# Weighted sums of attention heads made two pairs at a time in a hybrid decoder layer

## Chip, cores and metric

The kernel runs on one core of a Trainium2 chip. The metric is the device time of one execution in microseconds (us); before the change it is 390.96 us, the median of three runs (390.86 to 391.17).

## What is computed

One decoder layer over 512 positions of width 1024 in fp32. The input is normalized and projected to the queries, keys, values and gate paths of two attention branches, and to two merge gates. Branch A (8 heads of 64) is a block-sparse softmax attention with a relative bias; branch B (8 heads of 64) is stick-breaking attention. Each branch's output is multiplied by SiLU of its gate path, projected up to 1024, weighted with a sigmoid merge gate, and the sum goes through an output projection to which the input is added. Cut to what matters here:

```
oa = moba_attention(qa, ka, va, rel_bias)      # softmax weights x va, per head
ob = stick_breaking_attention(qb, kb, vb)      # stick-breaking weights x vb, per head
ya = (merge_heads(oa) * silu(za)) @ w_up_moba
yb = (merge_heads(ob) * silu(zb)) @ w_up_sb
y = sigmoid(gl_a) * ya + sigmoid(gl_b) * yb
x = x + y @ w_out
```

The change concerns the products "weights x values" of the heads, their place in the order of the work, and nothing of what they compute.

## The kernel before

The dense projections are products of fp32 split into a high and a low part, three matmuls for each piece (`mm3`, lines 177 to 181). The start of the kernel projects qa, ka, va and vb, row by row. From there on the main loop (lines 601 to 622) goes over eight pairs of heads, `PAIRS`: m = 0 to 3 are branch A, m = 4 to 7 branch B.

For a pair m the loop issues, in this order:

- `scores` (lines 407 to 421): 24 matmuls per pair for the two heads, 64 rows of the array each, so that the two heads stand side by side in the array (tile shape 64*128 in the profile). They go to six banks of PSUM of the kind "s".
- from m = 2 on, `finish(m - 1, "pj")`: the weighted sum of the pair before, in a bank of the kind "pj".
- for each of the two heads: `softmax` or `stick` on ScalarE (ACT) and VectorE (DVE), then `turn` (32x32 transposes on VectorE), `put` (four DMAs to DRAM), a `fill`, and `get` (a DMA back to SBUF, issued by ScalarE, into one of four buffers `pt`).
- two more `fill`s, with `finish(0)` between them at m = 1.

A `fill` takes the next entry of a list written out by hand (`FILLS`, lines 46 to 54): chunks of the dense projections, 24 matmuls over the whole array each (`chunk_ct`, lines 398 to 404), or a piece of branch A's up projection. They keep TensorE at work while a head's weights are made and turned. A fill's bank is of the kind "pj" where its tag says so; the first two fills of each m always are. Behind the last pair come two fills, `finish(7)`, one more fill, and branch B's up projection `up("b", c)`, which needs all of branch B's sums.

`finish(m, tag)` (lines 595 to 599) is `weighted` and `split_o`. `weighted` (lines 480 to 492) takes one bank `po`, issues eight matmuls, which the profile shows as 16, with 128 rows and 64 columns of the array each (tile shape 128*64), again the two heads side by side, and then one VectorE multiplication (line 491) that reads the bank and multiplies by SiLU of the gate path. `split_o` (lines 518 to 523) makes the high part on ScalarE (line 522) and the low part on VectorE (line 523). A finish issues no DMA.

There are two banks of the kind "pj" and six of the kind "s":

```python
BANKS = {"pj": 2, "s": 6}
...
def bank(tag, name):
    return pp.tile([P, S], F32, tag=tag, bufs=BANKS[tag], name=name)
```

A bank is used again only when whatever reads its last content is done. The framework puts each engine's instructions in a fixed order when the kernel is built: of those that are ready by its own reckoning of the times, the one that comes first in the source. On the chip each engine goes through its list in that order. So an instruction can stand behind others that come after it in the source.

Of the kernel before, what the change touches and what calls it, by code (L numbers as in the profile page):

```python
# [57 lines left out]
def hybrid_layer(ctx: ExitStack, tc: tile.TileContext, x, xT, w, rel, out):  # L58
# [40 lines left out]
    def sum_w(names, done):  # L99

        with tc.issue_after(G.tensor_copy(turn_of, done[:1, :1].bitcast(F32)).ins):  # L101
            for n in range(2):
                for name in names:
                    if n == 0:
                        sums[name] = vp.tile([P, H // 2, 2, P], F32, tag="v", name=name).rearrange("p a b d -> p (a b d)")
                    blk = TERMS[name[:2]][n]
                    src = sums[blk + name[2]] if blk[0] == "T" else w[WO + BLOCKS.index(blk + name[2])]
                    nc.gpsimd.dma_start(sums[name], src, **({"accum_op": ALU.add} if n else {}))
# [165 lines left out]
    def load_bias(h):  # L274
        bt = oms[2 + h % 2][:, :S]
        nc.sync.dma_start(bt, bass.AP(tensor=e_dr.tensor, offset=e_dr.offset + h * TW, ap=[[1, P], [1, S]]))
        return bt
# [129 lines left out]
    def scores(br, p, q, k, res):  # L407

        (qh, ql), (kh, kl) = q[p], k[p]
        for grp in ((3,), (2,), (1, 0)):  # L410
            ps = [bank("s", f"s{br}{2 * p + b}{grp[0]}") for b in range(2)]
            c = 0
            for i in grp:
                n = (i + 1) * P
                for m, (x, y) in enumerate(((qh, kl), (ql, kh), (qh, kh))):
                    for b in range(2):
                        o = slice(b * HD, (b + 1) * HD)
                        T.matmul(ps[b][:, c:c + n], x[o, i * P:(i + 1) * P], y[o, :n], start=m == 0, stop=m == 2)  # L418
                for b in range(2):
                    res[2 * p + b][i] = ps[b][:, c:c + n]  # L420
                c += n
# [32 lines left out]
    def turn(br, h, rows):  # L454
        turned = tp.tile([P, 4, BLK[-1], 32], F32, tag="turned", bufs=2, name=f"turned{br}{h}")
        for i in (3, 2, 1, 0):
            for j in range(0, i + 1, 2):
                n = min(2, i + 1 - j)
                step = (BLK[j + 1] - 1 - BLK[j]) if n == 2 else 1
                at = BLK[j] + i - j  # L460
                V.transpose(turned[:, :, at:at + (n - 1) * step + 1:step, :].rearrange("p q j r -> p j q r"),  # L461
                            rows[i][:, j * P:(j + n) * P].rearrange("p (j q c) -> p j q c", j=n, q=4))
        return turned

    def put(br, h, turned):
        dr = dp.tile([P, 4 * PQ], F32, tag="pd", bufs=4, name=f"pd{br}{h}")
        for a in range(4):
            nc.sync.dma_start(bass.AP(tensor=dr.tensor, offset=dr.offset + a * PQ,
                                      ap=[[4 * PQ, 32], [32 * 4 * PQ, 4], [1, PQ]]),
                              turned[a * 32:(a + 1) * 32].rearrange("c q k r -> c q (k r)"))  # L470
        return dr

    def get(br, h, dr):
        pt = tp.tile([P, 4 * PQ], F32, tag="pt", bufs=4, name=f"pt{br}{h}")
        nc.scalar.dma_start(pt, dr)
        return pt
# [3 lines left out]
    def weighted(tag, br, p, vv, pts):  # L480

        po = bank(tag, f"po{br}{p}")
        for j in range(NT):
            for b in range(2):
                o, c = slice(b * HD, (b + 1) * HD), (2 * p + b) * HD
                src = pts[b].rearrange("p (a n) -> p a n", a=4)[:, :, BLK[j] * 32:BLK[j + 1] * 32]
                T.matmul(po[o, :].rearrange("p (a n) -> p a n", a=4)[:, :, j * 32:], vv[j][:, c:c + HD], src,  # L487
                         start=j == 0, stop=j == NT - 1, skip_group_check=True)
        ocol[br, p] = u = slot(f"o{br}{p}")
        dst, z = (by_block((mirror if br == "a" else blocks)(x)) for x in (u, zr[br, p]))  # L490
        V.tensor_tensor(dst, po.rearrange("p (a i r) -> p a i r", a=4, i=4).rearrange("p a i r -> p i a r"), z,
                        op=ALU.mult)
# [25 lines left out]
    def split_o(br, p):  # L518
        u = ocol[br, p]
        oH[br, p] = slot(f"oh{br}{p}", F32R)  # L520
        oL[br, p] = slot(f"ol{br}{p}", F32R)
        A.activation(oH[br, p], u, AF.Copy)
        V.tensor_tensor(oL[br, p], u, oH[br, p].bitcast(F32), op=ALU.subtract)
# [59 lines left out]
    def fill(tag="pj"):  # L583

        home[0] = tag
        for kind, i in fills.pop(0):
            make[kind](i)

    PAIRS = [("a", p) for p in range(H // 2)] + [("b", p) for p in range(H // 2)]
    done = {}  # L590

    def head(m, b):
        return PAIRS[m][0], 2 * PAIRS[m][1] + b

    def finish(m, tag="s"):

        br, p = PAIRS[m]
        weighted(tag, br, p, v_of[br], [done.pop((m, b)) for b in range(2)])
        split_o(br, p)

    for m, (br, p) in enumerate(PAIRS):
        q, k = (qa, ka) if br == "a" else (qb, kb)
        sc, rw = {h: [None] * NT for h in (2 * p, 2 * p + 1)}, {h: [None] * NT for h in (2 * p, 2 * p + 1)}
        scores(br, p, q, k, sc)
        if m > 1:
            finish(m - 1, "pj")
        for b in range(2):
            h = 2 * p + b
            bias = load_bias(h) if br == "a" else None
            (softmax if br == "a" else stick)(h, sc[h], rw[h], bias, (3, 2, 1, 0))  # L610
            done[m, b] = put(br, h, turn(br, h, rw[h]))
            fill()
            if not b:
                done[m, 0] = get(*head(m, 0), done[m, 0])
        for b in range(2):
            if m == 1 and not b:
                finish(0)
            if not b:
                done[m, 1] = get(*head(m, 1), done[m, 1])
            if (m, b) in SUMS:  # L620
                sum_w(SUMS[m, b], done[m, b])
            fill("pj" if b or not fills[1] and m < len(PAIRS) - 1 else "s")
    fill()
    fill("s")
    finish(len(PAIRS) - 1)
    fill()
    assert not fills
# [163 lines left out]
```

## Time and profile before

| | |
|---|---|
| median of three runs | 390.96 us (390.86 to 391.17) |
| the profiled execution | 391.4 us, its span 389.6 us |
| TensorE matmul busy | 385.0 us, 99% of the span |
| VectorE busy | 266.8 us, 68% |
| ScalarE busy | 194.6 us, 50% |
| granted TensorE clock, mean | 0.999 |
| DMA, mean over the span | 203 GB/s |

Times in rows are microseconds from the span's start. PE is TensorE's matmuls, PEld its weight loads, DVE VectorE, ACT ScalarE. The ends of matmuls are modelled, so the time that a matmul costs is read from the start of one to the start of the next. In a timeline, a row is start, duration, engine, line, operation, result and operands, array tile, shape and count of merged instructions; in brackets the engine's idle time before it and what ended that.

### The profile page before, as it was taken

To read this page: it belongs to the slowest core of one execution; us is meant where nothing else is said; L and a number is where in the kernel's file an instruction comes from. 1 tells how busy PE (TensorE), PEld (TensorE's weight loads), DVE (VectorE), ACT (ScalarE), POOL (GpSimd) and SP (SyncE) were. 2 spreads that over 40 slices of the span, in tenths; PEclk is the share of its full clock that TensorE was granted. 3 is DMA by queue.
4 is the path that set the end of the run, shared out by engine and by line. 5 is a ranking of instruction groups with operands and counts; after the bars stand their busy time and mean duration, and the time that the engine had idled before them with its cause. 6 is when DMAs were issued, how large, how long until landed. Compare 5 with 4: busy or idle time off the path is not lost.

```text
span 389.6 us, 5321 instructions
## 1 busy us (share of the span) xinstructions
PE 385.0 (99%) x1853; PEld 308.8 (79%) x1853; DVE 266.8 (68%) x535; ACT 194.6 (50%) x341; POOL 51.9 (13%) x100
## 2 busy tenths in 40 slices
PE   8999999999999999999999999999999999999996
PEld 5888888888887878878788878878878878888885
DVE  4824995854879477295596398489459534999962
ACT  5684522945778466264552472363254232359540
POOL 1018966000000000000000100100000000232110
PEclk9999999999999999999999999999999999999999
DMA  7977259982496946827526776776772842798935
GB/s 266 330 269 241 112 157 290 307 273 73 133 259 226 295 178 151 306 74 240 175 68 192 257 202 182 246 205 170 263 215 67 271 148 89 217 245 301 196 76 175
DMA packets 36091, 79.29 MB, mean 203 GB/s; under 512 B 3929, under 2 KB 16729, under 8 KB 36065
## 3 DMA queue, kind: packets, MB, share of 16 engines
q1 hardware_dynamic: 29584, 56.68, 45.0%
q0 software_dynamic: 2880, 9.44, 10.6%
q10 hardware_dynamic: 3600, 12.85, 9.9%
q8 instruction: 14, 0.23, 0.2%
q14 instruction: 13, 0.10, 0.1%
HBM read 62.15 MB, written 14.70 MB: 197 GB/s over the span
## 4 chain that ended last, share of the span: by engine, by line
PE 99%; DVE 0%; issue 0%
PE gl L179 8%; PE gl L181 7%; PE gl L180 7%; PE poa L487 2%; PE pob L487 2%; PE sb L418 2%; PE sa L418 2%; PE za L179 2%; PE kb L179 2%; PE zb L179 2%; PE za L180 2%; PE kb L181 2%; PE zb L181 2%; PE zb L180 2%; PE yb L181 2%; PE yb L180 2%
## 5 line engine op out<-in xcount | busy, mean ns | idle before, releaser
L140 DVE TENSOR_TENSOR wl<-wr,wh 128x1024 fp32r<-128x1024 f32 (+1 forms) x64 | 75.8, 1185 | 62.1 <-ACT wh L138 57.0
L138 ACT ACTIVATE wh<-wr 128x1024 fp32r<-128x1024 f32 (+1 forms) x64 | 65.8, 1028 | 41.4 <-DMA wr<-in_w 15.8
L179 PE MATMUL gl<-xl,wh 128*128 128x512 f32 x128 | 50.5, 395 | 0.0
L181 PE MATMUL gl<-xh,wh 128*128 128x512 f32 x128 | 49.9, 390 | 0.0
L180 PE MATMUL gl<-xh,wl 128*128 128x512 f32 x128 | 49.8, 389 | 0.0
L513 ACT ACTIVATE gl<-gl,x 128x512 f32<-128x512 f32 x16 | 11.0, 690 | 41.7 <-PE gl L181 41.6
L179 PEld LDWEIGHTS gl<-xl,wh 128*128 128x128 f32 x128 | 24.0, 188 | 5.8 <-issue 1.0
L101 POOL COPY turn_of<-ptb 1x1 f32<-1x1 f32 x3 | 1.3, 433 | 202.0 <-DMA ptb<-pdb 202.0
L181 PEld LDWEIGHTS gl<-xh,wh 128*128 128x128 f32 x128 | 24.0, 188 | 5.1
L180 PEld LDWEIGHTS gl<-xh,wl 128*128 128x128 f32 x128 | 24.0, 188 | 4.8
L446 DVE TENSOR_TENSOR_SCAN sx<-om,begin 128x512 f32<-128x512 f32 (+3 forms) x32 | 24.9, 805 | 0.2 <-ACT om L442 0.2
L430 ACT ACTIVATE pa<-pa,m 128x512 f32<-128x512 f32 (+3 forms) x32 | 17.8, 557 | 10.9 <-DVE m L428 9.0
L428 DVE CUSTOM_DVE_ANT_0 pa<-sa,om 128x512 f32<-128x512 f32 (+3 forms) x32 | 14.8, 477 | 10.9 <-PE sa L418 10.9
L461 DVE STREAM_TRANSPOSE turneda<-pa 128x256 f32<-128x256 f32 (+1 forms) x48 | 16.4, 376 | 0.1
L442 ACT ACTIVATE om<-sb 128x512 f32<-128x512 f32 (+3 forms) x32 | 14.6, 462 | 3.2 <-DVE sx L446 2.9
L461 DVE STREAM_TRANSPOSE turnedb<-pb 128x256 f32<-128x256 f32 (+1 forms) x48 | 15.9, 370 | 0.0
L444 ACT ACTIVATE pb<-sb 128x512 f32<-128x512 f32 (+3 forms) x32 | 14.7, 465 | 0.0
L448 DVE TENSOR_TENSOR pb<-pb,sx 128x512 f32<-128x512 f32 (+3 forms) x32 | 14.2, 471 | 0.0
L179 PE MATMUL za<-xl,wh 128*128 128x512 f32 x32 | 12.7, 396 | 0.0
L179 PE MATMUL kb<-xl,wh 128*128 128x512 f32 x32 | 12.6, 393 | 0.0
L179 PE MATMUL zb<-xl,wh 128*128 128x512 f32 x32 | 12.6, 393 | 0.0
L181 PE MATMUL zb<-xh,wh 128*128 128x512 f32 x32 | 12.5, 390 | 0.0
(305 smaller groups left out, 957.9 us busy)
## 6 DMA issues: line engine op xcount, KB each, us to landing
wr<-in_w SPq DMA_DIRECT2D x60, 512.0 KB, 5.4
pda<-turneda SPq DMA_DIRECT2D x32, 160.0 KB, 2.6
pta<-pda ACTq DMA_DIRECT2D x8, 640.0 KB, 6.0
pdb<-turnedb SPq DMA_DIRECT2D x32, 160.0 KB, 2.7
ptb<-pdb ACTq DMA_DIRECT2D x8, 640.0 KB, 4.5
xn<-in_x SPq DMA_DIRECT2D x8, 256.0 KB, 6.6
xs<-in_xT SPq DMA_DIRECT2D x8, 256.0 KB, 6.2
om<-e_dr SPq DMA_DIRECT2D x8, 256.0 KB, 6.5
```

Source lines behind the costliest of these rows:

```text
L138: A.activation(hi[:, a:b], raw[:, a:b], AF.Copy)
L140: low[c] = V.tensor_tensor(lo[:, a:b], raw[:, a:b], hi[:, a:b].bitcast(F32), op=ALU.subtract).ins
L179: T.matmul(ps, aH, bL, start=start, stop=False, skip_group_check=on)
L180: T.matmul(ps, aL, bH, start=False, stop=False, skip_group_check=on)
L181: T.matmul(ps, aH, bH, start=False, stop=stop, skip_group_check=on)
L418: T.matmul(ps[b][:, c:c + n], x[o, i * P:(i + 1) * P], y[o, :n], start=m == 0, stop=m == 2)
L428: V.tensor_tensor_reduce(p, sc[i], bias[:, S - n:], scale=1.0, scalar=3e38, op0=ALU.add, op1=ALU.min, accum_out=m[:, 0:1])
L430: A.activation(p, p, AF.Exp, bias=m[:, 0:1], scale=-1.0, accum_out=m[:, 1:2])
L444: A.activation(p, z, AF.Sigmoid)
L446: V.tensor_tensor_scan(sx[:, n - 1::-1] if n == S else sx[:, :n][:, ::-1], om[:, e - n:][:, ::-1], begin[:, S - n:][:, ::-1], 0.0, op0=ALU ...
L461: V.transpose(turned[:, :, at:at + (n - 1) * step + 1:step, :].rearrange("p q j r -> p j q r"), rows[i][:, j * P:(j + n) * P].rearrange("p ...
L487: T.matmul(po[o, :].rearrange("p (a n) -> p a n", a=4)[:, :, j * 32:], vv[j][:, c:c + HD], src, start=j == 0, stop=j == NT - 1, skip_group ...
```

## The change

The weighted sums are no longer made one pair at a time behind the next pair's scores. At m = 2, 4 and 6, behind the scores of that pair, the sums of the two pairs before are made one behind the other, both in banks of the kind "pj". At m = 3, 5 and 7 there are none, the one inside m = 1 is gone, and the sums of pairs 6 and 7 are made together near the end, in banks of the kind "s".

```diff
         scores(br, p, q, k, sc)
-        if m > 1:
+        if m and m % 2 == 0:
+            finish(m - 2, "pj")
             finish(m - 1, "pj")
         for b in range(2):
             h = 2 * p + b
...
         for b in range(2):
-            if m == 1 and not b:
-                finish(0)
             if not b:
                 done[m, 1] = get(*head(m, 1), done[m, 1])
...
     fill()
     fill("s")
+    finish(len(PAIRS) - 2)
     finish(len(PAIRS) - 1)
     fill()
```

## Rows read from the trace of the kernel before

**Rows 1.** The page: busy us by engine, share of the span, instructions.
```profile
PE 385.0 (99%) x1853; PEld 308.8 (79%) x1853; DVE 266.8 (68%) x535; ACT 194.6 (50%) x341; POOL 51.9 (13%) x100
```

**Rows 2.** All of TensorE's waits: who waited for whom, total us, times, longest.
```profile
PE pwarm L172 <- DVE warm L86: 1.0, 1, 1.0
```

**Rows 3.** TensorE's timeline at m = 0: the scores' last matmuls, and the fill behind them.
```profile
94.62 0.27 PE L418 MATMUL sa<-ka0h,qa0h 64*128 64x128 f32 x2
...
95.17 0.39 PE L180 MATMUL za<-xh,wl 128*128 128x512 f32 x1
95.40 0.39 PE L181 MATMUL za<-xh,wh 128*128 128x512 f32 x1
```

**Rows 4.** TensorE's timeline at m = 6: scores, weighted sum of pair 5 (left out), fill.
```profile
256.16 0.27 PE L418 MATMUL sb<-kb2h,qb2h 64*128 64x128 f32 x2
...
258.67 0.50 PE L179 MATMUL gl<-xl,wh 128*128 128x512 f32 x1
259.00 0.39 PE L180 MATMUL gl<-xh,wl 128*128 128x512 f32 x1
```

**Rows 5.** TensorE's timeline near the end: fill, weighted sum of pair 7, fill.
```profile
317.60 0.39 PE L181 MATMUL gl<-xh,wh 128*128 128x512 f32 x1
317.92 2.37 PE L487 MATMUL pob<-ptb,vbs 128*64 128x512 f32 x16
320.23 0.50 PE L179 MATMUL gl<-xl,wh 128*128 128x512 f32 x1
320.56 0.40 PE L180 MATMUL gl<-xh,wl 128*128 128x512 f32 x1
```

**Rows 6.** Timeline of weight loads inside the weighted sum at m = 3.
```profile
166.36 0.20 PEld L487 LDWEIGHTS poa<-pta,vas 128*64 128x64 f32 x4
166.85 0.14 PEld L487 LDWEIGHTS poa<-pta,vas 128*64 128x64 f32 x2 [0.29 <-issue]
167.28 0.14 PEld L487 LDWEIGHTS poa<-pta,vas 128*64 128x64 f32 x2 [0.28 <-issue]
...
168.35 0.14 PEld L487 LDWEIGHTS poa<-pta,vas 128*64 128x64 f32 x2
```

**Rows 7.** Timeline: TensorE behind the sum at m = 2, then the multiplication.
```profile
142.29 0.50 PE L179 MATMUL gl<-xl,wh 128*128 128x512 f32 x1
...
143.99 0.66 DVE L491 TENSOR_TENSOR oa<-poa,za 128x512 f32<-128x512 f32 x1
```

**Rows 8.** The same at m = 4, then line 522, which reads the product.
```profile
195.04 0.50 PE L179 MATMUL kb<-xl,wh 128*128 128x512 f32 x1
...
197.47 0.66 DVE L491 TENSOR_TENSOR oa<-poa,za 128x512 f32<-128x512 f32 x1
...
198.16 0.64 ACT L522 ACTIVATE oha<-oa 128x512 fp32r<-128x512 f32 x1 [0.78 <-DVE oa L491]
```

**Rows 9.** VectorE and ScalarE at m = 6, timeline from the first scan to line 522.
```profile
256.64 2.07 DVE L446 TENSOR_TENSOR_SCAN sx<-om,begin 128x512 f32<-128x512 f32 x2
...
262.64 0.65 DVE L491 TENSOR_TENSOR ob<-pob,zb 128x512 f32<-128x512 f32 x1
...
263.33 0.63 ACT L522 ACTIVATE ohb<-ob 128x512 fp32r<-128x512 f32 x1 [1.22 <-DVE ob L491]
```

**Rows 10.** Timeline near the end: lines 491 and 523 of pair 7, branch B's up projection.
```profile
320.84 0.69 DVE L491 TENSOR_TENSOR ob<-pob,zb 128x512 f32<-128x512 f32 x1
...
322.22 0.69 DVE L523 TENSOR_TENSOR olb<-ob,ohb 128x512 fp32r<-128x512 f32 x1 [0.70 <-ACT ohb L522]
...
325.80 0.39 PE L179 MATMUL yb<-olb,wh 128*128 128x512 f32 x1
```

**Rows 11.** TensorE's timeline: the program's last matmul.
```profile
385.69 0.28 PE L181 MATMUL last<-wh,yh 128*128 128x256 f32 x1
```

**Rows 12.** Stretches behind it: length, busy PE, PEld, DVE, ACT, POOL, granted clock, DMA.
```profile
388.20:388.40 0.20, 0.00 (x0) 0.00 (x0) 0.00 (x0) 0.00 (x0) 0.00 (x0) 1.00 0.00 0
...
388.60:388.80 0.20, 0.00 (x0) 0.00 (x0) 0.00 (x0) 0.00 (x0) 0.00 (x0) 0.50 0.00 0
```

## The prediction

> **What bounds the kernel now.** I first read the page's busy times, to see which engine sets the end: TensorE is at work for 385.0 of 389.6 us [rows 1]. Then its waits: one of 1.0 us ahead of the warm-up, and no other [rows 2]. So TensorE never waits for data in the main loop, and any time is won only by giving it less to do and lost by making it wait even once. VectorE at 68% [rows 1] isn't the bound on average; whether it is late at one place, an average can't tell, so I read the timelines of the three engines around the weighted sums.
>
> What TensorE pays for a sum is read from starts. In steady fills one 512-wide matmul follows the last by 0.23 us [rows 3, 4]. From the last score matmul to the second matmul of the fill it takes 95.17 - 94.62 = 0.55 us without a sum [rows 3], and 259.00 - 256.16 = 2.84 us with one [rows 4]; m = 2 and m = 3 give 2.84 too. A sum behind the scores therefore costs 2.29 us. A sum between fills takes 320.56 - 317.60 = 2.96 us [rows 5], against two steps of 0.23 us without it: 2.50 us.
>
> What a sum costs inside, with no change of the array's tile shape, shows in its weight loads. After the first step (0.49 us) a step of two 512-wide matmuls takes 0.43 us [rows 6], and the sum has two each of 512, 384, 256 and 128 columns: 0.86 + 0.65 + 0.43 + 0.22 = 2.16 us. The rest, about 0.15 us behind scores and 0.34 us between fills, is the price of entering and leaving the shape 128*64.
>
> **The change, part by part.** *Removed and moved on TensorE.* Before, six sums stand behind scores and two between fills, and two pairs' scores go straight into a fill: 6 x 2.84 + 2 x 2.96 + 2 x 0.55 = 24.06 us. After, three double sums stand behind scores, one between fills, five scores go straight into a fill, and one place is plain fills (0.46 us): 3 x 2.84 + 2.96 + 5 x 0.55 + 0.46 = 14.69 us, and four second sums more. No row shows a sum right behind a sum. The bounds: 2.15 us, its 20 steps of 128 columns at the steady quarter of 0.43 us, if nothing is lost between the two, and the whole 2.31 us from a sum's start to the next work's start [rows 5], if the second bank and its values cost a fresh entry. I take 2.16 us, since the second sum has the shape of the first. The saving is 24.06 - 14.69 - 4 x 2.16 = **0.73 us**, between 0.77 and 0.13 us.
>
> It is five changes of shape fewer, at about 0.15 us each. The Trainium skill (TensorEngine Tiling (Array Packing), Key Properties) says that a change of tiling mode drains TensorE, which the rows bear out. For a drain of the array the Trainium skill (TensorE: Matmul & The Clock Gate, Step-by-step: what each phase is for) gives about 128 cycles; at 2.4 GHz that would be an estimated 0.053 us each and 0.27 us for five, less than half of what the rows give, and the sum goes by the rows.
>
> *Moved on VectorE and ScalarE.* Each sum takes along one multiplication (line 491), one copy (line 522) and one subtraction (line 523). No DMA is in it, and it passes no DMA of SP's or POOL's queue. The buffers `pt` are held for two pairs at most, which is the four there are; the next `get` that needs one comes after a head's weights are made, turned and put, behind the sums that free it. At m = 3, 5 and 7 VectorE has less to do, which TensorE, not waiting for it there, doesn't feel: nothing. Near the end the last subtraction starts at 322.22 and branch B's up projection at 325.80 [rows 10], so a second set of line 491, 522 and 523 (0.69 us or less each) stays hidden by the fill between: nothing. If that fill were not there, it would cost up to 2 us.
>
> *The wait that is added.* Here the two banks of the kind "pj" matter. Before, a sum takes one and the first fill behind it the other; the fill after that, more than 5 us later (24 matmuls of 0.23 us), needs the sum's bank. After, the two sums take both banks, so the first fill behind them has to wait until the multiplication of the first sum has read its bank. TensorE has only the second sum to do meanwhile, 2.16 us; behind the waiting matmul stands all its other work.
>
> When does that multiplication come? It precedes the head's softmax in the source, but in the trace it stands behind many of those instructions on VectorE, since VectorE's order was fixed by a reckoning in which the sum ended later than it does. At m = 2 the sum is over at 142.29 and the multiplication at 143.99 + 0.66 = 144.65 [rows 7]; at m = 4 at 195.04, and line 522, which reads it, starts at 198.16 [rows 8]; at m = 6 at 258.67 [rows 4], and line 522 starts at 263.33 [rows 9], because from 256.64 on VectorE works through the first head's scans, products and transposes without a pause. (m = 5 and m = 7 look like m = 6: the multiplication starts 3.95 and 4.03 us after the sum, there 3.97 us.) The place of line 491 against the scores should stay, since scores, first sum and softmax of the same m are unchanged. Then the fill waits
>
> - at m = 2: 144.65 - (142.29 + 2.16) = 0.20 us
> - at m = 4: 198.16 - (195.04 + 2.16) = 0.96 us
> - at m = 6: 263.33 - (258.67 + 2.16) = 2.50 us
>
> together **3.66 us**. Below, the bound is nothing, if the order on VectorE is another; above, m = 4 may be as late as m = 6 (1.5 us more). The second multiplication is late next: its bank is wanted by the second fill, 5.5 us after the first began. With its start some 4 to 5 us behind the first multiplication that fits narrowly; I add nothing and up to 0.5 us for the upper bound.
>
> *Sum.* -0.73 + 3.66 = +2.93 us against the profiled execution's own 391.4 us, so 394.3 us there; that execution lies 0.4 us over the median of 390.96, so **393.9 us** as a median. The forecast's own range is 392.6 to 395.6 us.
>
> **The rivals.** *No wait: the order on VectorE shifts* (faster or no change). If the multiplication comes within 1.5 us of the first sum's end, the fill finds its bank free: 2.16 us less its 0.66 us. In its favour, near the end it comes after 0.61 us [rows 5, 10], and a new order is made for the changed kernel. Against it, near the end VectorE has no head's weights to make, and at m = 4 and 6 it has. It gives 390.96 - 0.73 = 390.2 us. That is 0.19%, and with the bounds of the saving 390.2 to 390.8 us.
>
> *Half the wait.* The planner puts line 491 a few instructions sooner at m = 6, or fills the gap with a fill in another kind of bank, so that some 1.3 us remain: 390.96 - 0.73 + 1.3 = 391.5 us, on either side of no measurable change.
>
> *More than the sum.* TensorE's granted clock is at 1.00 (2.4 GHz) throughout, and after the last matmul at 385.69 it is still so at 388.20 and at 0.50 (1.2 GHz) from 388.60 [rows 11, 12]. The wait at m = 6 comes close to such an idle time. If the clock fell there, the fill behind it could take up to another 5.5 us; or the second fill waits as well. This gives 396 to 399 us. Against it, the wait forecast is shorter than the idle time before that fall.
>
> **How the numbers follow.** A difference under 0.2% (0.8 us) can't be told from no change by a measurement of this kernel. The forecast gets 0.62: what it rests on, two banks and VectorE's order, is in the code and in four loops of the trace, but the order is made anew. No wait gets 0.16, half the wait 0.14, more than the sum 0.08. No wait lies at the edge of 0.2%: I give 0.09 of it to faster and 0.07 to the same; half the wait gives 0.08 to the same and 0.06 to slower. So faster 0.09, same 0.15, slower 0.76. For the range, leaving out both "no wait" and "more" would leave out over 0.2; so it reaches from 390.2 us to 395.6 us.
>
> **What would show it.** Right, if TensorE's waits in the changed kernel show two or three waits for line 491 in front of the first fill at m = 2, 4 and 6, about 0.2, 1.0 and 2.5 us long; if a second sum starts 2.2 us behind the first; if scores at odd m go into a fill in 0.55 us, and the sums near the end cost no wait. The prediction is wrong if the multiplication of the first sum stands ahead of the scans at m = 4 and 6, or if TensorE does other work in its place; the saving is wrong if two sums take over 4.6 us.

## The result, and the profile after

The change makes the kernel slower: 396.35 us (median of four executions, 395.01 to 396.69) against 391.02 us before (median of four executions, 390.86 to 391.17), a ratio of 1.0124 with a 95% interval from 1.0112 to 1.0136. The execution whose trace is read here is the fastest of the four (395.01 us, span 393.2 us, mean granted clock 1.00); the other three took 396.2 to 396.7 us with a mean clock of 0.994 to 0.996, which a second trace explains further down.

TensorE's busy time is what it was, 384.9 us against 385.0 us [rows 1], and two waits for the multiplication of a weighted sum, line 491, have come in where there was none [rows 2]. TensorE's waits in the changed kernel (who waited for whom, total us, times, longest):

```profile
PE gl L179 <- DVE ob L491: 2.5, 1, 2.5
PE pwarm L172 <- DVE warm L86: 1.0, 1, 1.0
PE kb L179 <- DVE oa L491: 0.6, 1, 0.6
PE qa L206 <- ACT wh L138: 0.4, 1, 0.4
```

The last row stands in the projections at the start; the first scores begin at 92.79 us, against 92.76 us before, so it costs nothing here. The table doesn't hold all of it: a wait can also show at the weight loads, and at m = 2 it does. So I read the timeline of the changed kernel at the four double sums, each from the start of the sum (the row with x32) to the first matmul of the fill behind it. Near the end, where nothing is waited for, that takes 323.82 - 319.37 = 4.45 us:

```profile
319.37 4.53 PE L487 MATMUL pob<-ptb,vbs 128*64 128x512 f32 x32
...
322.28 0.69 DVE L491 TENSOR_TENSOR ob<-pob,zb 128x512 f32<-128x512 f32 x1
...
323.82 0.50 PE L179 MATMUL gl<-xl,wh 128*128 128x512 f32 x1
```

At m = 6 it takes 262.47 - 255.40 = 7.07 us, 2.62 us more. VectorE goes through the first head's work from 255.67 on, as in [rows 9], and comes to the multiplication at 261.67; the second one, at 264.74, holds nobody up:

```profile
255.40 4.53 PE L487 MATMUL pob<-ptb,vbs 128*64 128x512 f32 x32
...
255.67 2.07 DVE L446 TENSOR_TENSOR_SCAN sx<-om,begin 128x512 f32<-128x512 f32 x2
...
261.67 0.65 DVE L491 TENSOR_TENSOR ob<-pob,zb 128x512 f32<-128x512 f32 x1
...
262.47 0.47 PE L179 MATMUL gl<-xl,wh 128*128 128x512 f32 x1 [2.55 <-DVE ob L491]
...
264.74 0.69 DVE L491 TENSOR_TENSOR ob<-pob,zb 128x512 f32<-128x512 f32 x1
```

At m = 4 it takes 196.38 - 191.23 = 5.15 us, 0.70 us more, since the multiplication comes a little sooner than in [rows 8]:

```profile
191.23 4.53 PE L487 MATMUL poa<-pta,vas 128*64 128x512 f32 x32
...
195.65 0.68 DVE L491 TENSOR_TENSOR oa<-poa,za 128x512 f32<-128x512 f32 x1
...
196.38 0.50 PE L179 MATMUL kb<-xl,wh 128*128 128x512 f32 x1 [0.62 <-DVE oa L491]
```

At m = 2 it takes 143.13 - 137.50 = 5.63 us, 1.18 us more, and not for the multiplication, which is in time at 140.98. The second sum's weight loads wait for the fetch of pair 1's second head (pta<-pda). ScalarE issued it at 135.67, behind an evacuation of a fill (line 513) that had waited 3.80 us for that fill's last matmul:

```profile
135.53 0.69 ACT L513 ACTIVATE gl<-gl,x 128x512 f32<-128x512 f32 x1 [3.80 <-PE gl L181]
...
135.67 0.33 ACTq L475 DMA_DIRECT2D pta<-pda  x1
...
137.50 5.70 PE L487 MATMUL poa<-pta,vas 128*64 128x512 f32 x32
...
140.83 0.20 PEld L487 LDWEIGHTS poa<-pta,vas 128*64 128x64 f32 x4 [0.99 <-DMA pta<-pda]
140.98 0.65 DVE L491 TENSOR_TENSOR oa<-poa,za 128x512 f32<-128x512 f32 x1
...
143.13 0.50 PE L179 MATMUL gl<-xl,wh 128*128 128x512 f32 x1
```

Before the change the same fetch stood one fill earlier on ScalarE. The timeline there:

```profile
132.59 0.69 ACT L513 ACTIVATE gl<-gl,x 128x512 f32<-128x512 f32 x1 [3.56 <-PE gl L181]
...
132.81 0.33 ACTq L475 DMA_DIRECT2D pta<-pda  x1
```

This accounts for the traced execution. A second sum behind a first costs 4.45 - 2.31 = 2.14 us, so the changes of tile shape give back 24.06 - 14.69 - 4 x 2.14 = 0.81 us. The waits cost 1.18 + 0.70 + 2.62 = 4.50 us. That makes +3.69 us; the span went from 389.6 to 393.2 us, +3.6 us.

### The profile page after: what moved, and what is told of

Same layout as the page of the kernel before. It is cut to its first block, busy times and chain, and to the rows that moved or that the text cites. A ratio compares the mean times of both kernels' runs of the same rounds, so it can differ in the third digit from the quotient of the medians.

```text
span 393.2 us, 5338 instructions
## 1 busy us (share of the span) xinstructions
PE 384.9 (98%) x1853; PEld 308.9 (79%) x1853; DVE 267.3 (68%) x535; ACT 199.5 (51%) x345; POOL 51.9 (13%) x100
## 4 chain that ended last, share of the span: by engine, by line
PE 85%; DMA 6%; DVE 4%; ACT 3%; issue 1%; ACTq 0%; DVEq 0%; SPq 0%
PE gl L179 6%; PE gl L180 6%; PE gl L181 6%; DMA wr<-in_w 3%; PE kb L179 2%; PE zb L179 2%; PE kb L180 2%; PE ya L181 2%; PE kb L181 2%; PE zb L180 2%; PE yb L181 2%; PE yb L180 2%; PE ya L180 2%; PE zb L181 2%; PE vb L179 2%; PE va L181 2%
## 5 line engine op out<-in xcount | busy, mean ns | idle before, releaser
L180 PE MATMUL kb<-xh,wl 128*128 128x512 f32 x32 | 12.5, 390 | 0.0
```

The costliest lines, as they stand in the source:

```text
L180: T.matmul(ps, aL, bH, start=False, stop=False, skip_group_check=on)
```

## The experiments

Theory: the loss is made of three things: line 491 late on VectorE at m = 4 and 6, a fetch late on ScalarE at m = 2, and TensorE's granted clock, which in most executions falls behind the long wait at m = 6. To compare kernels at m = 6 I use the time from the first score matmul of m = 6 to that of m = 7: 31.81 us before the change (254.30 to 286.11), 33.95 us with a second sum and no wait (31.81 + 2.14), 36.56 us in the changed kernel's first trace:

```profile
253.33 0.50 PE L418 MATMUL sb<-kb2l,qb2h 64*128 64x512 f32 x2
...
289.89 0.50 PE L418 MATMUL sb<-kb3l,qb3h 64*128 64x512 f32 x2
```

**The changed kernel once more** (no edit).

> The changed kernel once more, for a trace of an execution in which the granted clock is under 1.00. Theory (clock falls behind the 2.6 us wait at m = 6): most executions show a mean granted clock of 0.994 to 0.996 and 396.2 to 396.7 us, some 1.00 and 395.0 us; in a trace of the former the clock is at 0.50 for some 3 us shortly behind that wait and nowhere else. Rival (other disturbance): the low clock stands elsewhere, or the time is lost in longer waits with the clock at 1.00.

Measured: 397.08 us (395.11 to 397.32), ratio 1.0133 (1.0108 to 1.0159); three of four executions had a clock of 0.994 to 0.996, the fourth, with 0.998, took 395.11 us. The trace, taken in one with 0.994, has the same wait of 2.5 us for line 491. The stretches behind it (length; busy PE, PEld, DVE, ACT, POOL; granted clock; DMA):

```profile
260.00:262.00 2.00, 0.65 (x8) 0.29 (x4) 2.00 (x7) 1.39 (x6) 0.00 (x0) 1.00 1.02 195
...
263.00:264.00 1.00, 0.81 (x4) 0.71 (x5) 1.00 (x3) 0.63 (x1) 0.00 (x0) 1.00 0.04 8
264.00:265.00 1.00, 1.00 (x5) 0.82 (x4) 1.00 (x3) 0.00 (x0) 0.00 (x0) 0.83 0.76 181
265.00:266.00 1.00, 1.00 (x4) 0.77 (x3) 1.00 (x2) 0.00 (x0) 0.00 (x0) 0.50 0.94 218
...
267.00:268.00 1.00, 1.00 (x3) 0.73 (x3) 1.00 (x3) 0.00 (x0) 0.00 (x0) 0.50 0.00 0
268.00:270.00 2.00, 2.00 (x10) 1.64 (x9) 2.00 (x7) 0.00 (x0) 0.00 (x0) 0.98 0.00 0
```

TensorE stands idle until 263.2; the clock falls from 1.00 to 0.50 (2.4 to 1.2 GHz) shortly after it has resumed, and is back at 268. After that it stays at 1.00 until the last matmul. From scores to scores m = 6 takes 38.15 us instead of 36.56: the fall costs 1.6 us.

```profile
254.05 0.50 PE L418 MATMUL sb<-kb2l,qb2h 64*128 64x512 f32 x2
...
292.20 0.50 PE L418 MATMUL sb<-kb3l,qb3h 64*128 64x512 f32 x2
```

The expectation holds, with one addition: fetches cost more here than in the first trace. At m = 4 the time from the sums to the fill is 5.55 us instead of 5.15, since the second sum waits for the fetch of pair 3's second head, issued behind line 309; at m = 2 it is 5.84 us instead of 5.63. In the first trace the fetch at m = 4 was issued at 189.41 and landed 3.8 us later, in time; here it took 5.0 us:

```profile
189.77 0.33 ACTq L475 DMA_DIRECT2D pta<-pda  x1
...
194.85 0.20 PEld L487 LDWEIGHTS poa<-pta,vas 128*64 128x64 f32 x4 [0.91 <-DMA pta<-pda]
```

**Two sums together at m = 6 alone.**

```diff
-        if m and m % 2 == 0:
-            finish(m - 2, "pj")
-            finish(m - 1, "pj")
+        if m > 1 and m != 5:
+            if m == 6:
+                finish(m - 2, "pj")
+            finish(m - 1, "pj")
```

(`finish(0)` is back inside m = 1, and the end has `finish(7)` alone.)

> Two sums together at m = 6 alone, all others as before the change. Theory: one change of shape fewer (-0.15 us) and the wait for the first multiplication at m = 6 (+2.6 us), so 393.4 us with the clock at 1.00, and some 1.4 us more, 394.9 us, in executions in which the clock falls behind that wait; most do. Rival (the clock falls for another reason, or the waits of m = 2 and 4 are needed for it): 393.4 us and a clock of 1.00 in all executions.

Measured: 395.23 us (394.91 to 395.68), ratio 1.01 (1.0083 to 1.0117), the clock 0.994 to 0.996 in all four executions; the time is 0.3 us over the 394.9 us expected with a fall. So m = 6 by itself brings the clock down, without the other waits. Here it falls earlier than in the trace above: a mean of 0.62 from 260 to 262 means some 1.5 us at 0.50, so it fell near 260.5, when TensorE was still waiting; the first matmul behind the wait already takes 0.77 us instead of 0.47. TensorE's longest wait, that matmul, and three stretches from the end of the wait on:

```profile
PE gl L179 <- DVE ob L491: 2.5, 1, 2.5
```

```profile
260.80 0.77 PE L179 MATMUL gl<-xl,wh 128*128 128x512 f32 x1 [2.55 <-DVE ob L491]
```

```profile
260.00:262.00 2.00, 1.20 (x3) 1.04 (x4) 2.00 (x5) 0.63 (x1) 0.00 (x0) 0.62 0.18 38
262.00:263.00 1.00, 1.00 (x3) 0.79 (x3) 1.00 (x2) 0.00 (x0) 0.00 (x0) 0.50 0.92 205
...
264.00:265.00 1.00, 1.00 (x6) 0.82 (x5) 1.00 (x2) 0.43 (x1) 0.00 (x0) 1.00 0.40 111
```

**Two sums together everywhere but at m = 6.**

```diff
-        if m and m % 2 == 0:
+        if m in (2, 4):
             finish(m - 2, "pj")
+        if m in (2, 4, 5, 6):
             finish(m - 1, "pj")
```

> Two sums together at m = 2, at m = 4 and at the end, but one at m = 5 and one at m = 6. Theory: -0.65 us for the changes of shape, +1.2 us for the late fetch at m = 2, +0.7 us for the multiplication at m = 4: 392.3 us, the clock at 1.00 in all executions, no wait over 1.3 us. Rival (the clock falls with any double sum): 393.5 us or more with a clock under 1.00.

Measured: 392.60 us (392.02 to 393.79 in ten executions), ratio 1.0033 (1.0024 to 1.0043), no clock under 0.998. The rival falls: a double sum and its shorter waits leave the clock alone. The median is 0.3 us over the expectation, and the weight loads in the timeline show why: at m = 4 too the second sum waits for a fetch.

```profile
140.58 0.20 PEld L487 LDWEIGHTS poa<-pta,vas 128*64 128x64 f32 x4 [1.10 <-DMA pta<-pda]
...
194.13 0.20 PEld L487 LDWEIGHTS poa<-pta,vas 128*64 128x64 f32 x4 [0.82 <-DMA pta<-pda]
```

**The multiplication moved ahead on VectorE.** `finish` returns the multiplication, and the work for the weights is queued behind it:

```diff
+        first = None
...
-            finish(m - 2, "pj")
+            first = finish(m - 2, "pj")
...
-            (softmax if br == "a" else stick)(h, sc[h], rw[h], bias, (3, 2, 1, 0))
+            make_w = softmax if br == "a" else stick
+            if not b:
+                make_w(h, sc[h], rw[h], bias, (3,))
+            with tc.issue_after(first) if first else nullcontext():
+                make_w(h, sc[h], rw[h], bias, (2, 1, 0) if not b else (3, 2, 1, 0))
```

> The changed kernel, with VectorE's work for the head's weights, all but that of the first tile, queued behind the first sum's multiplication at m = 2, 4 and 6. Theory (VectorE's order makes the waits at m = 4 and m = 6): both waits are gone, the clock is 1.00 in all executions, only the late fetch at m = 2 is left: 391.0 - 0.8 + 1.2 = 391.4 us. Rival (the two banks hold TensorE up whatever VectorE's order, or delayed softmax work makes sums or fills late elsewhere): waits of 1 us or more for line 491 remain or new waits come, 393 us or more.

Measured: 391.83 us (390.82 to 392.25 in ten executions), ratio 1.0013 (1.0003 to 1.0022), no clock under 0.998. (A mean of 0.998 is no fall in the loop: the trace was taken in an execution that has it, and there the clock is under 1.00 only behind the last matmul.) In the timeline at m = 6 the multiplication now follows one scan and one product, 3.0 us after the sums began, and the fill follows the sums after 4.46 us without a wait:

```profile
254.88 4.53 PE L487 MATMUL pob<-ptb,vbs 128*64 128x512 f32 x32
...
257.90 0.65 DVE L491 TENSOR_TENSOR ob<-pob,zb 128x512 f32<-128x512 f32 x1
...
259.34 0.50 PE L179 MATMUL gl<-xl,wh 128*128 128x512 f32 x1
```

So with two banks it was VectorE's order that made TensorE wait; no run changed the number of banks. From scores to scores m = 6 takes 33.97 us. What is left is m = 2, 1.40 us in this trace, for the fetch; 391.24 - 0.81 + 1.40 is just the time measured.

**The fetches moved ahead on ScalarE as well.** On top of the kernel above (`got` holds the issued fetches by head):

```diff
-        A.activation(g, ps, AF.Sigmoid, bias=mb[:, i:i + 1])
+        with tc.issue_after(got["a", 3]) if i == 2 else nullcontext(): A.activation(g, ps, AF.Sigmoid, bias=mb[:, i:i + 1])
...
-        A.activation(hi, ps, AF.Copy, scale=scale)
+        with tc.issue_after(got["a", 7]) if name == "qb1" else nullcontext(): A.activation(hi, ps, AF.Copy, scale=scale)
```

> The kernel mult_first, with two evacuations on ScalarE (line 513 of gate 2, line 309 of qb1) queued behind the fetches of the second heads of pairs 1 and 3, so that these fetches are issued before the last fill of m = 1 and m = 3 ends. Theory (late fetches because ScalarE waits ahead of them): no wait of TensorE for a fetch or for line 491 is left, and only the changes of shape show: 391.2 - 0.8 = 390.4 us with the clock at 1.00, 0.2% faster than before the change. Rival (the fetch is late because its data are, or the saving by the changes of shape isn't real): 391.2 us or more.

Measured: 390.42 us (389.94 to 390.81 in eleven executions) against 391.17 us, ratio 0.9979 (0.9969 to 0.9988). TensorE's waits are again the one of the start; the timeline at m = 2 shows the fetch 3.3 us ahead of the evacuation that held it up, and the fill 4.46 us behind the start of the sums:

```profile
PE pwarm L172 <- DVE warm L86: 1.0, 1, 1.0
```

```profile
131.99 0.33 ACTq L475 DMA_DIRECT2D pta<-pda  x1
135.33 0.69 ACT L513 ACTIVATE gl<-gl,x 128x512 f32<-128x512 f32 x1 [3.80 <-DMA wr<-in_w]
...
137.29 4.53 PE L487 MATMUL poa<-pta,vas 128*64 128x512 f32 x32
...
141.75 0.50 PE L179 MATMUL gl<-xl,wh 128*128 128x512 f32 x1
```

This version is the fastest of all: 0.75 us, or 0.2%, under the kernel before (0.5 to 1.2 us by the interval). With no wait left in its trace, what remains of the change is the saving by fewer changes of shape. From the first scores to the last matmul the two traces differ by 0.91 us: 385.69 - 92.76 = 292.93 us before, 384.60 - 92.58 = 292.02 us here.

**The fetches alone**, with VectorE's order left to the planner.

> The changed kernel, with the two fetches put ahead of the evacuations on ScalarE and VectorE's order left to the planner. Theory: the waits for fetches at m = 2 and m = 4 go (-1.2 to -2.3 us), the wait for line 491 at m = 6 stays at 2.6 us with the clock falling behind it in most executions: 394.7 to 395.5 us, 393.8 us where the clock stays at 1.00. Rival (the fetches are hidden behind the wait for line 491 and cost nothing of their own): 396.4 us or more.

Measured: 394.38 us (393.34 to 394.93), ratio 1.0072 (1.0055 to 1.0088); 393.34 us was the execution with the clock at 1.00, the others had 0.993 to 0.996. The fetch waits are gone (from the sums to the fill it takes 4.46 us at m = 2 and m = 4), so they cost their own time: the rival falls. It is 0.3 to 0.5 us under the expectation because the planner, given another order on ScalarE, also put line 491 at m = 4 sooner, at 192.77, where it holds nobody up (the first fill starts at 194.71). The wait at m = 6 stays:

```profile
PE gl L179 <- DVE ob L491: 2.5, 1, 2.5
```

**A shorter wait at m = 6.** The kernel with both orders, but at m = 6 the first head's three larger tiles stay free, ahead of the multiplication:

```diff
-            if not b:
-                make_w(h, sc[h], rw[h], bias, (3,))
+            free = (() if b else (3, 2, 1) if m == 6 else (3,))
+            make_w(h, sc[h], rw[h], bias, free)
             with tc.issue_after(first) if first else nullcontext():
-                make_w(h, sc[h], rw[h], bias, (2, 1, 0) if not b else (3, 2, 1, 0))
+                make_w(h, sc[h], rw[h], bias, [i for i in (3, 2, 1, 0) if i not in free])
```

> The kernel both, but at m = 6 with the multiplication of the first sum behind three tiles of the first head's work, so that TensorE waits there for about 1.9 us. Theory: 390.4 + 1.9 = 392.3 us as long as the clock stays at 1.00, and about 1.4 us more in executions in which it falls; with a wait shorter than that at m = 6 of the changed kernel, I expect it to fall in under half of the executions. Rival (any wait of 1.9 us brings the clock down): 393.7 us and a granted clock of 0.996 or less in all.

Measured: 393.30 us (392.82 to 393.99), ratio 1.0054 (1.004 to 1.0069). Two executions had a clock of 0.998 and 1.00 and took 392.82 and 392.98 us, two had 0.996 and took 393.63 and 393.99 us. So the fall came in half of the executions, not in under half, and the rival, a fall in all of them, doesn't hold either. The trace was taken in the one of 393.63 us and has a wait of 2.0 us and a fall behind it:

```profile
252.98 4.53 PE L487 MATMUL pob<-ptb,vbs 128*64 128x512 f32 x32
...
258.74 0.65 DVE L491 TENSOR_TENSOR ob<-pob,zb 128x512 f32<-128x512 f32 x1
...
259.54 0.47 PE L179 MATMUL gl<-xl,wh 128*128 128x512 f32 x1 [2.03 <-DVE ob L491]
```

```profile
258.00:260.00 2.00, 0.46 (x2) 0.45 (x3) 2.00 (x6) 0.95 (x4) 0.00 (x0) 0.98 0.77 150
260.00:261.00 1.00, 1.00 (x4) 0.75 (x3) 1.00 (x2) 0.39 (x3) 0.00 (x0) 0.50 0.00 0
```

```profile
250.91 0.50 PE L418 MATMUL sb<-kb2l,qb2h 64*128 64x512 f32 x2
...
288.52 0.50 PE L418 MATMUL sb<-kb3l,qb3h 64*128 64x512 f32 x2
```

From scores to scores m = 6 takes 37.61 us here, 3.64 us more than the 33.97 us of the kernel with both orders. The wait is 2.10 us of that (259.54 - 252.98 = 6.56 us from the sums to the fill, less 4.46), and the fall the other 1.54 us, about what was expected. The four times alone would put a fall at 0.9 us, but they are two against two, and the time from the start to the first scores varies almost as much, from 92.26 to 92.98 us in the nine traces. The executions without a fall are 0.5 to 0.7 us over the expected 392.3 us; no trace of one was taken, so the reason stays open.

## Why the prediction was right and where it failed

- *TensorE bounds, so each wait shows in full, and the new wait is for line 491 in front of the first fill:* right. The waits at m = 4 and m = 6 came where they were forecast and are made by VectorE's order, as mult_first shows. At m = 6 the term was 2.50 us and measured 2.62; at m = 4 it was 0.96 and measured 0.70.
- *The saving by fewer changes of shape:* right, 0.81 us instead of 0.73, since a second sum costs 2.14 us and not 2.16. The kernel "both", whose trace has no added wait, is 0.75 us faster. The Trainium skill (TensorE: Matmul & The Clock Gate, Step-by-step: what each phase is for) gives about 128 cycles for a drain; at 2.4 GHz five would be an estimated 0.27 us. The measurement, 0.15 to 0.18 us for each change (0.75 to 0.91 us for five), decides.
- *The `get`s cost nothing:* this step failed. I asked whether a fetch would lack a buffer and whether the moved sums pass a queue, and not whether ScalarE's list would be put in another order. It was: the fetch of pair 1's second head came to stand behind an evacuation that waits for a fill to end, so it was issued at 135.67 instead of 132.81. The wait that I put at 0.20 us at m = 2, for line 491, was 1.18 us, for that fetch. In other executions m = 4 had a fetch wait too.
- *The clock:* the sum had no term for it, and the rival that had one, "more than the sum", got a chance of 0.08. This is the step that failed most. I set that rival aside because the forecast wait was shorter than the idle time before the fall behind the program's last matmul [rows 11, 12]. But that is one fall in one execution, and hardly a longer idle time: the matmul ends at 385.97 by the profile and the clock is down by 388.60, at most 2.6 us against a forecast wait of 2.50. With a wait of 2.6 us at m = 6 the mean clock was 0.996 or less in 13 of 16 executions, and the fall costs 1.5 to 1.6 us in the three of these that were traced. What I named as that rival's time, 396 us and more, is what came, though not by the clock alone: the late fetch is part of it.
- *The end, and the second multiplication:* right; neither cost a wait.
- *The sum:* for the traced execution I had 394.3 us and it took 395.0. The late fetch makes +0.98 of that, line 491 at m = 4 and 6 together -0.14, the saving -0.08, which is +0.76. For the median I had 393.9 us and it is 396.35: the clock adds 1.34 (396.35 - 395.01), and the rest of some 0.3 us is the difference between profiled execution and median, which I carried over from the kernel before. It took both failed steps to leave the range of 390.2 to 395.6 us: the two executions of the changed kernel without a fall took 395.01 and 395.11 us, and without the late fetches, with the clock falling in three of four executions, the median was 394.38 us (gets_first, where the wait of 0.70 us at m = 4 is gone too).

Open: why the clock falls in some executions of one kernel and not in others. A longer wait than 2.6 us wasn't tried, and every wait of 2.0 us or more stood at m = 6, so the length of the wait and its place aren't told apart.

## What to carry to other kernels

When a change makes an engine that never waits depend on a second buffer of a pool of two, look up in the trace where the instruction that frees the buffer stands on its own engine, not where it stands in the source; its lateness there is a price that was hidden until now. When the order is made by a planner, a moved step can reorder lists that it doesn't touch, as here the fetches that ScalarE issues: pin the freeing instruction and the fetches ahead of the work that may wait, and the saving that the change was made for comes through. A wait of TensorE of some two microseconds in a dense stretch may cost more than its own length, here some 1.5 us more, so the clock belongs into the sum and not only into the rivals.

## What was not expected of the hardware

TensorE's clock fell behind waits as short as 2.0 us (two executions of four), and behind those of 2.6 us in 13 of 16; in the four traces that have the fall it cost 1.45 to 1.6 us on top of the wait. In the 31 executions of the three kernels whose traces show no wait over 1.4 us in the main loop (not_m6, mult_first, both), the mean clock was never under 0.998. The fall needn't come within the wait: in only_m6 it came some 0.3 us before the matmuls began again, in the changed kernel's second trace more than a microsecond after. And the changed kernel's first trace has the wait of 2.5 us with the clock at 1.00 throughout, while six of the kernel's eight executions show a fall by their mean clock: one trace at full clock doesn't show that a wait is harmless.
